# Holding back the splits of the last expert's weights in layer 1 of a two-layer trunk

## The chip, the cores and the metric

The kernel runs on one core of a Trainium2 chip. A core has a matrix engine (TensorE, PE in the profile, with its weight loads listed as PEld), a vector engine (VectorE, DVE), a scalar engine (ScalarE, ACT), a general engine (GpSimd, POOL) and SyncE (SP), which here does nothing but issue transfers. Each works through its own list of instructions in the order of the program. They meet at semaphores, and 16 DMA engines move data between the large memory and the on-chip memory. The metric is the device time of one execution in microseconds (us), as a median of several runs.

## The reference, cut to what matters

Two layers, each a token mixer (attention and gating branches) followed by a mixture of 16 experts. The experts part, for 512 latent and 256 context tokens:

```python
def ec_moe(h, w_r, w1, w3, w2):
    aff = jax.nn.softmax((h @ w_r).astype(jnp.float32), axis=-1)
    gate, idx = lax.top_k(jnp.swapaxes(aff, 1, 2), cap)      # each expert picks its tokens
    xin = jax.vmap(lambda hb, ib: hb[ib])(h, idx)
    hid = jax.nn.silu(jnp.einsum('becd,edf->becf', xin, w1)) * jnp.einsum('becd,edf->becf', xin, w3)
    ye = jnp.einsum('becf,efd->becd', hid, w2) * gate[..., None].astype(h.dtype)
    return jax.vmap(lambda yb, ib: jnp.zeros((n, D), h.dtype).at[ib.reshape(-1)].add(yb.reshape(-1, D)))(ye, idx)
```

The three matrices of an expert are 1024 x 1024 in float32. An expert takes 64 latent and 32 context tokens, 96 rows in all.

## The kernel before, in words

The change lies in `experts_quad`, the experts of the first layer. Each expert's matrices come in as 24 tiles of 128 x 1024 floats (512 KB), eight for each of w_e1, w_e3 and w_e2. The tiles are fetched in one fixed sequence: w_e1 of expert e+1, then w_e2 of expert e, then w_e3 of expert e+1, and so on. So the sequence ends with eight tiles of w_e2 of expert 14, eight of w_e3 of expert 15 and eight of w_e2 of expert 15. `moe_load` issues them from SP as buffers come free. A transfer on SP also waits until the transfer eight places ahead of it has landed, since eight semaphores take turns.

For experts 0 to 14 the loop runs `stage_1(e+1)` (the product with w_e1, 96 matmuls recorded as 192, then a Silu on ACT, line 1329), `stage_h(e)` (the hidden activations of expert e are transposed on PE, line 1316, and copied from PSUM by two ACT copies, line 1323), `stage_2(e)` (the product with w_e2 on PE, line 1267; three gate multiplications on DVE, line 1342, each followed by a scatter that adds its quarter rows to the token table `x1a` from POOL, line 1344), and `stage_3(e+1)` (the product with w_e3, then a multiplication on DVE, line 1335). The three scatters of an expert go one after the other, since all of them add into `x1a`.

The last expert, number 15, is treated apart, because its result is taken straight into the next layer. Its hidden activations are kept as a pair of reduced-precision parts (`fp32r`, high and low): ACT copies the high part from PSUM (line 1320), and DVE subtracts to get the low part (line 1321). Its eight w_e2 tiles are split the same way by `split_w`: a CAST on ACT (line 153) makes the high part and a subtraction on DVE (line 155) the low part, so one tile costs one instruction on each. `mm_rows` (line 1276) then runs six matmuls for a tile: high by high twice, high by low twice, low by high twice. The splits use the tag `w` with six buffers, so three tiles can be split ahead of their matmuls. Around this `stage_x` loads a row of numbers (`k<-in_iota`, line 1364), compares it on DVE (line 1368, called hot below) and reloads `x1a` in six pieces (line 1372). `settle` (line 1381) then adds the last expert by a matmul with that comparison. The next layer begins there, with four early loads of its `w_in` tiles into buffers `y`, `y`, `m`, `m`.

The order on each engine is made by a scheduler that runs ahead of time: an instruction that has what it needs early in its estimate is put early, though written later in the code. `tc.issue_after(ins)` makes the instructions of a block stand behind `ins` on the engine of `ins`; other engines and the waits on data are left alone.

Of the kernel before, what the change touches and what calls it, by code (L numbers as in the profile page):

```python
# [38 lines left out]
def fr(ap):  # L39
    return ap.bitcast(F32)  # L40
# [68 lines left out]
class Trunk:  # L109
# [1145 lines left out]
    def experts_quad(self, l):  # L1255
        nc = self.nc
# [3 lines left out]
        state, got = {}, {}  # L1260
# [9 lines left out]

        def mm_rows(ps, hT, name, e):
            for k in range(KD):
                w = self.moe_w((name, l, e, k))
                for i, (a, b) in enumerate(self.PAIRS):
                    for hf in range(2):
                        nc.tensor.matmul(ps[:, hf * 512:(hf + 1) * 512], lhsT=hT[a][:, k, :],
                                         rhs=w[b][:, hf * 512:(hf + 1) * 512],
                                         start=(k == 0 and i == 0), stop=(k == KD - 1 and i == 2))
# [25 lines left out]
        def stage_h(e, final):  # L1304
            x = state.pop(("s", e))
            if final:
                pair = [self.tl([P, 4, 2, M], F32R, "k3") for _ in range(2)]
                state["h", e] = [v.rearrange("p q f m -> p (q f) m") for v in pair]
            else:
                hT = self.tl([P, 4, 2, M], F32, "k3")  # L1310
                state["h", e] = hT.rearrange("p q f m -> p (q f) m")
            for f in range(2):
                tp = self.p1([P, 3, P])
                for r in range(3):
                    c0 = r * QW + f * P
                    nc.tensor.transpose(tp[:, r, :], x[:, c0:c0 + P], self.ident)
                v = tp.rearrange("p r (q m) -> p q r m", q=4)
                o = lambda t: t[:, :, f, :].rearrange("p q (r m) -> p q r m", r=3)
                if final:
                    nc.scalar.copy(o(pair[0]), v)  # L1320
                    nc.vector.tensor_tensor(out=o(pair[1]), in0=v, in1=fr(o(pair[0])), op=ALU.subtract)
                else:
                    nc.scalar.copy(o(hT), v)  # L1323
# [23 lines left out]
        def stage_2_rows(e):  # L1347
            ps = self.p2([M, D])
            mm_rows(ps, state.pop(("h", e)), "w_e2", e)
            y = self.tl([M, D], F32, "tg")  # L1350
            for hs in (slice(0, BW), slice(BW, D)):
                nc.vector.scalar_tensor_tensor(out=y[:, hs], in0=ps[:, hs], scalar=self.gate[:M, e:e + 1], in1=self.gtr[:M, hs],
                                               op0=ALU.mult, op1=ALU.mult)
            ys = state["y"] = [self.tl([P, D], F32R, "w") for _ in range(2)]
            for hs in (slice(0, BW), slice(BW, D)):
                nc.scalar.copy(ys[0][:M, hs], y[:, hs])
                nc.vector.tensor_sub(ys[1][:M, hs], y[:, hs], fr(ys[0][:M, hs]))
            nc.gpsimd.indirect_dma_start(out=dst[:, :], out_offset=bass.IndirectOffsetOnAxis(ap=self.idx[:M, e:e + 1], axis=0),
                                         in_=y, in_offset=None, compute_op=ALU.add)
# [34 lines left out]
        for e in range(NEXP):  # L1394
            final = e == NEXP - 1
            if not final:
                stage_1(e + 1)
            stage_h(e, final)
            if final:
                stage_x()  # L1400
                stage_2_rows(e)
            else:
                stage_t(e + 2)
                gather(e + 3)
                stage_2(e)
                stage_3(e + 1)
# [314 lines left out]
```

## Time and profile before

| | us |
|---|---|
| median of 3 runs | 2679.74 |
| lowest, highest of them | 2674.07, 2679.84 |
| the profiled execution | 2676.03 |
| span of its instructions | 2674.3 |
| mean granted clock of TensorE, share of full | 0.967 |

The page says for each engine how long it was busy and how often. It then cuts the span into 40 slices of 66.9 us and gives each engine's busy share in tenths. The later views list, for a window, who waited for whom, or the instructions in order of time; an idle time in square brackets names what ended it. Times count from the first instruction of the span.

### The profile page before, as it was taken

The page shows a single profiled execution, that of the slowest core. Times are in us where ns is not written, and L with a number is a line of the kernel's source. Part 1 is how long each engine was busy: PE and PEld are TensorE (multiplying, and loading weights), DVE is VectorE, ACT ScalarE, POOL GpSimd, SP SyncE. Part 2 cuts the span into 40 slices and gives each one's busy share as a digit, 9 for nine tenths or more (in the row PEclk, how much of TensorE's full clock was granted, in tenths as well). Part 3 has the DMA queues.
Part 4 walks back from the last instruction along what each step waited for, and adds up shares of the span by engine and source line. Part 5 has one row for each costly group of instructions (what it writes and reads, how often), then busy time and mean ns, then how long its engine had stood idle before and what let it go on. Part 6 is the DMA issues. An engine that isn't in the chain of part 4 may idle for free.

```text
span 2674.3 us, 47343 instructions
## 1 busy us (share of the span) xinstructions
PE 2448.9 (92%) x19598; PEld 1681.8 (63%) x19598; DVE 1224.4 (46%) x2457; ACT 804.0 (30%) x1729; POOL 190.5 (7%) x188
## 2 busy tenths in 40 slices
PE   7989999999999879999996899999999969988886
PEld 5888877777778746666664587888788843211111
DVE  7767776878696431111111455657765341100002
ACT  4556455444623300000000355534453220000000
POOL 0000000001000011111111100000000011000100
PEclk9999999999999989999998899999999979999999
DMA  7674664342246779999999353252223689999998
GB/s 281 197 231 150 209 208 135 121 146 94 78 146 236 267 284 383 390 386 382 382 385 391 113 173 119 76 166 71 80 78 121 209 336 401 407 408 407 407 406 333
DMA packets 194264, 654.59 MB, mean 245 GB/s; under 512 B 22720, under 2 KB 32960, under 8 KB 194048
## 3 DMA queue, kind: packets, MB, share of 16 engines
q1 hardware_dynamic: 174928, 610.32, 62.3%
q0 software_dynamic: 13696, 27.53, 4.2%
q10 hardware_dynamic: 5424, 13.70, 1.8%
q8 instruction: 154, 2.52, 0.4%
q14 instruction: 62, 0.51, 0.1%
HBM read 615.03 MB, written 25.95 MB: 240 GB/s over the span
## 4 chain that ended last, share of the span: by engine, by line
PE 62%; DMA 20%; DVE 10%; ACT 4%; issue 2%; POOL 1%; SPq 0%; ACTq 0%; POOLq 0%; DVEq 0%
PE p L327 22%; PE p L1267 18%; PE p L467 5%; DMA h<-in_w_e 4%; PE p L1429 4%; PE p L1094 3%; DMA w<-in_w_e 2%; PE p L492 2%; DMA raw<-in_w_in 2%; DVE w L155 2%; DMA q<-q 2%; DMA e<-in_w_e 2%; DMA raw<-in_w_e 2%; DMA m<-in_w_e 2%; PE p L609 1%
## 5 line engine op out<-in xcount | busy, mean ns | idle before, releaser
L327 PE MATMUL p<-h,w 128*128 128x512 f32 (+1 forms) x4416 | 916.4, 358 | 12.3 <-DVE w L155 5.6
L327 PEld LDWEIGHTS p<-h,w 128*128 128x128 f32 x4416 | 709.1, 191 | 131.4 <-issue 7.5
L155 DVE TENSOR_TENSOR w<-raw,w 128x1024 fp32r<-128x1024 f32 x224 | 273.4, 1222 | 227.4 <-ACT w L153 218.3
L153 ACT CAST w<-raw 128x1024 fp32r<-128x1024 f32 x224 | 235.0, 1050 | 374.0 <-PE p L327 140.1
L1267 PE MATMUL p<-h,k 128*32 128x256 f32 x3744 | 205.7, 379 | 0.0
L467 PE MATMUL p<-y,w 128*128 128x512 f32 (+1 forms) x864 | 177.3, 362 | 1.1 <-DVE w L155 1.1
L1267 PEld LDWEIGHTS p<-h,k 128*32 128x32 f32 x3744 | 120.4, 110 | 81.4 <-issue 1.5
L264 DVE SCALAR_TENSOR_TENSOR w<-raw,raw 128x1024 bf16<-128x1024 f32 x128 | 155.7, 1220 | 22.9 <-DMA raw<-in_w_adaT 16.1
L167 POOL TENSOR_TENSOR st<-st,mhalf 128x1 f32<-128x1 f32 x76 | 55.5, 730 | 1544.2 <-DVE st L165 1264.0
L467 PEld LDWEIGHTS p<-y,w 128*128 128x128 f32 x864 | 144.6, 191 | 28.2 <-DVE w L155 1.5
L1329 ACT ACTIVATE v<-p 128x768 f32<-128x768 f32 x16 | 13.0, 812 | 427.0 <-PE p L1267 427.0
L492 PE MATMUL p<-k,q 128*128 128x256 f32 (+1 forms) x576 | 109.5, 320 | 25.7 <-DMA q<-q 15.6
L1429 PE MATMUL p<-h,k 128*64 128x512 f32 x444 | 113.2, 622 | 16.8 <-DMA h<-in_w_e 15.7
L492 PEld LDWEIGHTS p<-k,q 128*128 128x128 f32 x576 | 85.4, 195 | 41.3 <-issue 10.7
L1267 PE MATMUL p<-raw,k 128*32 128x256 f32 x1560 | 88.5, 383 | 21.0 <-ACT k L1323 21.0
L1344 POOL DMA_INDIRECT x1a<-tg,idx x45 | 69.8, 1550 | 440.8 <-DVE tg L1342 238.5
L1462 ACT COPY k<-p 128x256 f32<-128x256 f32 x32 | 10.4, 375 | 297.6 <-PE p L1442 297.6
L1094 PE MATMUL p<-w,h 128*128 128x512 f32 x384 | 91.3, 395 | 1.6 <-DVE w L155 1.1
L1474 DVE TENSOR_TENSOR w<-w,p 128x512 f32<-128x512 f32 x16 | 11.0, 687 | 163.5 <-PE p L1429 152.3
L1429 PEld LDWEIGHTS p<-h,k 128*64 128x64 f32 x444 | 26.2, 137 | 94.6 <-DMA h<-in_w_e 57.4
L1267 PEld LDWEIGHTS p<-raw,k 128*32 128x32 f32 x1560 | 50.5, 111 | 55.2 <-ACT k L1323 21.2
L1335 DVE TENSOR_TENSOR v<-v,p 128x768 f32<-128x768 f32 x16 | 15.3, 954 | 149.4 <-PE p L1267 140.3
(340 smaller groups left out, 3038.0 us busy)
## 6 DMA issues: line engine op xcount, KB each, us to landing
h<-in_w_e SPq DMA_DIRECT2D x267, 512.0 KB
raw<-in_w_in SPq DMA_DIRECT2D x164, 512.0 KB
raw<-in_w_e SPq DMA_DIRECT2D x115, 512.0 KB
e<-in_w_e SPq DMA_DIRECT2D x93, 512.0 KB
y<-in_w_e SPq DMA_DIRECT2D x88, 512.0 KB
m<-in_w_e SPq DMA_DIRECT2D x84, 512.0 KB
raw<-in_w_adaT SPq DMA_DIRECT2D x80, 512.0 KB
w<-in_w_e SPq DMA_DIRECT2D x54, 512.0 KB
```

Source lines behind the costliest of these rows:

```text
L153: nc.scalar.copy(hi, fr(raw))
L155: nc.vector.tensor_sub(lo, fr(raw), fr(hi))
L167: nc.gpsimd.tensor_tensor(out=r, in0=v, in1=self.mhalf, op=ALU.pow)
L264: nc.vector.scalar_tensor_tensor(out=dump, in0=fr(raw), scalar=1.0, in1=self.cb[v], op0=ALU.mult, op1=ALU.mult, accum_out=self.mod[s, l][: ...
L327: nc.tensor.matmul(ps, lhsT=w[a][:, k * P:(k + 1) * P], rhs=h[k][:, b, :], start=(k == 0 and i == 0), stop=(k == KD - 1 and i == 2))
L467: nc.tensor.matmul(bps, lhsT=wb[a][:, (jj * 4 + k) * P:(jj * 4 + k + 1) * P], rhs=y[k][:, b, :], start=(k == 0 and i == 0), stop=(k == 3 a ...
L492: nc.tensor.matmul(ps, lhsT=Q[:, h, i, qs], rhs=k, start=(i == 0), stop=(i == 1))
L609: nc.tensor.matmul(ypsd[pr][64 * hh:64 * hh + 64, b * P:(b + 1) * P], lhsT=V[vi][:, head * 64:(head + 1) * 64], rhs=pT[hh][:, j * P:(j + 1 ...
L1094: nc.tensor.matmul(banks[i][hf], lhsT=c.mh[k][:, a, i * P:(i + 1) * P], rhs=w[b][:, hf * BW:(hf + 1) * BW], start=(k == 0 and p == 0), sto ...
L1267: nc.tensor.matmul(ps[32 * q:32 * q + 32, r * QW:(r + 1) * QW], lhsT=xT[:, k, 32 * r:32 * r + 32], rhs=w[:, q * QW:(q + 1) * QW], start=(k ...
L1344: nc.gpsimd.indirect_dma_start(out=dst4, out_offset=bass.IndirectOffsetOnAxis(ap=self.idx4[:, r, e:e + 1], axis=0), in_=y[:, r, :], in_off ...
L1429: nc.tensor.matmul(ps[half(h), :], lhsT=xT[:, k, :], rhs=w[:, h * BW:(h + 1) * BW], start=(k == 0), stop=(k == KD - 1))
```

## The change

The split of the last expert's w_e2 tiles is traced inside `issue_after` with the last of the two ACT copies of that expert's high part:

```diff
         def mm_rows(ps, hT, name, e):
             for k in range(KD):
-                w = self.moe_w((name, l, e, k))
+                with self.tc.issue_after(state["after"]):
+                    w = self.moe_w((name, l, e, k))
...
                 if final:
-                    nc.scalar.copy(o(pair[0]), v)
+                    state["after"] = nc.scalar.copy(o(pair[0]), v).ins
                     nc.vector.tensor_tensor(out=o(pair[1]), in0=v, in1=fr(o(pair[0])), op=ALU.subtract)
```

The line numbers after the first hunk are one higher in the changed kernel. On ACT, in the kernel before, from the copies of expert 13's hidden activations (`k_2472`) to the fourth split; `v_14916` is the Silu of expert 15, `k_2503` the copies of expert 14, `k_2509` those of expert 15, and `w_15164`, `w_15174`, `w_15184` the high parts of the last expert's first three tiles:

```order
L1323 COPY k_2472_14547<-p_2474_14553 128x4x96
L153 CAST w_15164<-m_14754 128x1024
L153 CAST w_15174<-y_14768 128x1024
L153 CAST w_15184<-y_14782 128x1024
L1329 ACTIVATE v_14916<-p_2497_14811 128x768
L1323 COPY k_2503_14918<-p_2504_14919 128x4x96
L1323 COPY k_2503_14918<-p_2505_14924 128x4x96
L1320 CAST k_2509_15131<-p_2511_15133 128x4x96
L1320 CAST k_2509_15131<-p_2512_15139 128x4x96
L153 CAST w_15194<-y_14796 128x1024
```

And the same stretch of ACT in the changed kernel:

```order
L1324 COPY k_2472_14547<-p_2474_14553 128x4x96
L1330 ACTIVATE v_14916<-p_2497_14811 128x768
L1324 COPY k_2503_14918<-p_2504_14919 128x4x96
L1324 COPY k_2503_14918<-p_2505_14924 128x4x96
L1321 CAST k_2509_15131<-p_2511_15133 128x4x96
L1321 CAST k_2509_15131<-p_2512_15139 128x4x96
L153 CAST w_15164<-m_14754 128x1024
L153 CAST w_15174<-y_14768 128x1024
L153 CAST w_15184<-y_14782 128x1024
L153 CAST w_15194<-y_14796 128x1024
```

Three CASTs moved from ahead of expert 15's Silu to behind the last expert's copies. On DVE, in the kernel before, from expert 14's `stage_3` multiplication (`v_14545`) on; `tg_15026` are the gate multiplications that feed the scatters of expert 14, `k_2514` is hot:

```order
L1335 TENSOR_TENSOR v_14545<-v_14545,p_2488_14697 128x768
L155 TENSOR_TENSOR w_15166<-m_14754,w_15164 128x1024
L155 TENSOR_TENSOR w_15176<-y_14768,w_15174 128x1024
L155 TENSOR_TENSOR w_15186<-y_14782,w_15184 128x1024
L1342 SCALAR_TENSOR_TENSOR tg_15026<-p_2506_14929,gate_114,q_8562 128x256 x3
L1335 TENSOR_TENSOR v_14916<-v_14916,p_2508_15033 128x768
L1321 TENSOR_TENSOR k_2510_15132<-p_2511_15133,k_2509_15131 128x4x96
L1321 TENSOR_TENSOR k_2510_15132<-p_2512_15139,k_2509_15131 128x4x96
L155 TENSOR_TENSOR w_15196<-y_14796,w_15194 128x1024
L1368 TENSOR_SCALAR k_2514_15147<-k_2513_15145,st_15148 96x768
L155 TENSOR_TENSOR w_15206<-y_14812,w_15204 128x1024
```

And in the changed kernel:

```order
L1336 TENSOR_TENSOR v_14545<-v_14545,p_2488_14697 128x768
L1343 SCALAR_TENSOR_TENSOR tg_15026<-p_2506_14929,gate_114,q_8562 128x256 x3
L1336 TENSOR_TENSOR v_14916<-v_14916,p_2508_15033 128x768
L1322 TENSOR_TENSOR k_2510_15132<-p_2511_15133,k_2509_15131 128x4x96
L1322 TENSOR_TENSOR k_2510_15132<-p_2512_15139,k_2509_15131 128x4x96
L155 TENSOR_TENSOR w_15166<-m_14754,w_15164 128x1024
L155 TENSOR_TENSOR w_15176<-y_14768,w_15174 128x1024
L1369 TENSOR_SCALAR k_2514_15147<-k_2513_15145,st_15148 96x768
L155 TENSOR_TENSOR w_15186<-y_14782,w_15184 128x1024
L155 TENSOR_TENSOR w_15196<-y_14796,w_15194 128x1024
```

Hot stood behind four splits and stands behind two. On SP, in the kernel before, from the last two w_e2 tiles on:

```order
L147 DMA e_14854<-in_w_e 128x1024
L147 DMA y_15254<-in_w_in 128x1024
L147 DMA y_15256<-in_w_in 128x1024
L147 DMA m_15258<-in_w_in 128x1024
L1372 DMA e_15151<-x1a 128x1024
L1372 DMA raw_15153<-x1a 128x1024
L1372 DMA raw_15155<-x1a 128x1024
L1372 DMA raw_15157<-x1a 128x1024
L1364 DMA k_2513_15145<-in_iota 96x768
L1372 DMA raw_15159<-x1a 128x1024
L1372 DMA raw_15161<-x1a 128x1024
L147 DMA m_15260<-in_w_in 128x1024
```

And in the changed kernel:

```order
L147 DMA e_14854<-in_w_e 128x1024
L1373 DMA e_15151<-x1a 128x1024
L1373 DMA raw_15153<-x1a 128x1024
L1373 DMA raw_15155<-x1a 128x1024
L1373 DMA raw_15157<-x1a 128x1024
L1365 DMA k_2513_15145<-in_iota 96x768
L1373 DMA raw_15159<-x1a 128x1024
L1373 DMA raw_15161<-x1a 128x1024
L147 DMA y_15254<-in_w_in 128x1024
L147 DMA y_15256<-in_w_in 128x1024
L147 DMA m_15258<-in_w_in 128x1024
L147 DMA m_15260<-in_w_in 128x1024
```

Three loads of the next layer's `w_in`, which reuse buffers of the tiles being split, moved from ahead of the `x1a` loads to behind them. On PE eight small transposes of the next layer (line 174) stand between the matmuls of `mm_rows` and no longer behind them; on POOL nothing moved.

## Rows read from the trace of the kernel before

**Rows 1.** The head of the page and the busy shares of PE in 40 slices.

```profile
span 2674.3 us, 47343 instructions
...
PE   7989999999999879999996899999999969988886
```

**Rows 2.** Who waited for whom from 1445 to 1520 us: in total us, how often, the longest.

```profile
ACT w L153 <- DMA m<-in_w_e: 48.4, 1, 48.4
...
PE p L1267 <- ACT k L1323: 21.0, 1, 21.0
...
DVE k L1368 <- DMA k<-in_iota: 6.8, 1, 6.8
...
PE p L1276 <- DVE w L155: 5.9, 1, 5.9
```

**Rows 3.** ACT in order of time, around experts 13 and 14: start us, duration us, line, operation, names, and in brackets the idle time ahead and what ended it.

```profile
1415.44 0.81 ACT L1329 ACTIVATE v<-p 128x768 f32<-128x768 f32 x1 [31.02 <-PE p L1267]
...
1465.42 1.04 ACT L153 CAST w<-m 128x1024 fp32r<-128x1024 f32 x1 [48.42 <-DMA m<-in_w_e]
...
1467.87 1.04 ACT L153 CAST w<-y 128x1024 fp32r<-128x1024 f32 x1 [0.17 <-DMA y<-in_w_e]
1468.82 0.81 ACT L1329 ACTIVATE v<-p 128x768 f32<-128x768 f32 x1
1469.52 0.85 ACT L1323 COPY k<-p 128x384 f32<-128x384 f32 x2
1494.07 0.86 ACT L1320 CAST k<-p 128x384 fp32r<-128x384 f32 x2 [23.70 <-PE p L1316]
...
1515.07 1.04 ACT L153 CAST w<-y 128x1024 fp32r<-128x1024 f32 x1
```

**Rows 4.** PE in order of time, in the same columns, from expert 13's transposes to the end of the last expert's product.

```profile
1415.30 0.87 PE L1316 MATMUL p<-ident,v 128*128 128x128 f32 x6
...
1416.98 3.23 PE L1267 MATMUL p<-h,k 128*32 128x256 f32 x56
...
1448.19 0.87 PE L1316 MATMUL p<-ident,v 128*128 128x128 f32 x6
1470.05 2.79 PE L1267 MATMUL p<-raw,k 128*32 128x256 f32 x24 [20.98 <-ACT k L1323]
...
1494.60 6.25 PE L1276 MATMUL p<-w,k 128*96 128x512 f32 x26 [0.29 <-ACT k L1320]
1506.70 6.96 PE L1276 MATMUL p<-w,k 128*96 128x512 f32 x22 [5.86 <-DVE w L155]
```

**Rows 5.** The chain of work that ended last, from 1440 to 1510 us: start us, us, what.

```profile
1447.20 10.74 DMA h<-in_w_e
...
1458.01 9.84 DMA y<-in_w_e
...
1498.05 6.83 DMA k<-in_iota
```

**Rows 6.** The transfers of line 147 issued from SP between 1440 and 1480 us: duration of the issue (ns, least, median, most), and the starts of the first and the last.

```profile
L147 SPq DMA_DIRECT2D m<-in_w_e x4: 327/328/328, 1451.0 to 1455.5; - x4
L147 SPq DMA_DIRECT2D y<-in_w_e x4: 327/328/328, 1456.7 to 1460.5; - x4
L147 SPq DMA_DIRECT2D e<-in_w_e x3: 327/327/328, 1461.8 to 1464.2; - x3
```

**Rows 7.** DVE in order of time, in the columns of rows 3.

```profile
1427.61 1.27 DVE L1342 SCALAR_TENSOR_TENSOR tg<-p,gate,q 128x256 f32<-128x256 f32 x3 [8.67 <-PE p L1267]
1438.04 0.95 DVE L1335 TENSOR_TENSOR v<-v,p 128x768 f32<-128x768 f32 x1 [9.16 <-PE p L1267]
...
1482.01 1.27 DVE L1342 SCALAR_TENSOR_TENSOR tg<-p,gate,q 128x256 f32<-128x256 f32 x3 [11.84 <-PE p L1267]
1492.42 0.95 DVE L1335 TENSOR_TENSOR v<-v,p 128x768 f32<-128x768 f32 x1 [9.15 <-issue]
```

**Rows 8.** The scatters of line 1344 on POOL in order of time, in the columns of rows 3, and last the time of all 45 from issue to landing (us, least, median, most).

```profile
1428.50 1.54 POOL L1344 DMA_INDIRECT x1a<-tg,idx  x1 [14.51 <-DVE tg L1342]
1437.38 1.54 POOL L1344 DMA_INDIRECT x1a<-tg,idx  x1 [7.34 <-DMA x1a<-tg,idx]
1446.02 1.54 POOL L1344 DMA_INDIRECT x1a<-tg,idx  x1 [7.09 <-DMA x1a<-tg,idx]
1482.77 1.54 POOL L1344 DMA_INDIRECT x1a<-tg,idx  x1 [35.21 <-DVE tg L1342]
1487.33 1.54 POOL L1344 DMA_INDIRECT x1a<-tg,idx  x1 [3.02 <-DMA x1a<-tg,idx]
1492.31 1.54 POOL L1344 DMA_INDIRECT x1a<-tg,idx  x1 [3.44 <-issue]
...
DMA to landing us min/median/max: 3.8/7.9/8.7
```

**Rows 9.** The first transfer that SP issued after 1495 us.

```profile
1496.19 0.33 SPq L1372 DMA_DIRECT2D e<-x1a  x1
```

**Rows 10.** Stretches of the program: their length, busy us of PE, PEld, DVE, ACT and POOL with counts, the granted clock of TensorE (1.00 is full), the share of the DMA engines, and GB/s.

```profile
1505.00:1510.00 5.00, 3.30 (x8) 2.26 (x9) 4.93 (x5) 1.04 (x1) 0.00 (x0) 0.50 0.63 257
...
1565.00:2000.00 435.00, 424.26 (x2479) 353.31 (x2479) 272.19 (x545) 210.43 (x506) 12.89 (x20) 1.00 0.34 106
```

## The prediction, made before the result was known

> **What bounds the kernel now.** I read the head of the page first. PE is busy in nearly every slice, so time is won only where PE itself stands still. The slice from 1404 to 1471 us shows a 6 between nines [rows 1]. I then asked who waited for whom around it: PE waited 21.0 us for an ACT copy, and ACT had waited 48.4 us for a weight tile, a wait far longer than any of the others; later PE waited 5.9 us for a split on DVE, and DVE 6.8 us for `k<-in_iota` [rows 2].
>
> ACT in order of time tells the rest. Expert 14's Silu started 0.14 us after expert 13's transposes on PE had begun (1415.30 to 1415.44) [rows 3, 4]. Expert 14's transposes began at 1448.19, but expert 15's Silu started at 1468.82. Ahead of it stood three CASTs whose tiles came in at 1465.4 to 1467.9 [rows 3, 4]. The Silu needed none of them. The tiles are the first three of the last expert's w_e2, which PE wants only at 1494.60. So the wait is a queue on ACT and not the weights of the product that PE was to do next.
>
> Are those weights there? A transfer issued at 1447.20 let the one at 1458.01 go, eight places on, and that one landed at 1467.85; so eight tiles take 9.84 to 10.74 us, about 1.29 us a tile [rows 5]. The first split tile is the last of four `m` loads [rows 6] and was there at 1465.42 [rows 3]. Counted back by 1.29, the eighth tile of w_e3 of expert 15 is there at 1464.1 and its first at 1455.1, and w_e2 of expert 14 from 1444.8 to 1453.8. All of these were issued while PE stood, so PE's progress does not set them.
>
> **The change part by part.** *The Silu goes ahead.* It can start at 1448.19 + 0.14 = 1448.33. From Silu to the first matmul takes 1470.05 - 1468.82 = 1.23 us [rows 3, 4], so PE begins expert 14's w_e2 product at 1449.56, 20.49 us earlier. It uses a tile every 1.3 us, the eighth at about 1458.7 and the eighth of w_e3 at about 1469: both at least 4.9 us after they land. From start to gate multiplication took 10.63 us for expert 13 (1416.98 to 1427.61) and 11.96 us for expert 14 (1470.05 to 1482.01) [rows 4, 7]; PE ran slower for the first microseconds after its long idle. Without the idle I take 10.63: 1460.19. In the same way the w_e3 product's multiplication, 21.06 us after the start (1416.98 to 1438.04), comes at 1470.62 where it came at 1492.42 [rows 4, 7]. That step alone gains 21.8 us.
>
> *The splits lose their head start.* Three CASTs of 1.04 us now follow the copies. The copies start 1494.07 - 1492.42 = 1.65 us after the multiplication [rows 3, 7], at 1472.27, and last 0.86 us; the first matmul then waits for a CAST, until 1474.2 instead of 1472.8. That is 1.4 us, and the first low part needs some 1.2 us more on DVE. The eight small transposes now fill part of it; where they stood they lay under DVE's gate multiplication and cost nothing. All this is hidden by the next wait; without that cover it would cost 2.6 us.
>
> *The row of numbers becomes the bound.* Hot on DVE stands behind two splits now. Everything from the third low part on waits for `k<-in_iota`. That load is behind the `x1a` loads on SP, and the first of those waits for the third scatter of expert 14. The chain goes: gate multiplication 1460.19; first scatter 0.89 us later (1427.61 to 1428.50 [rows 7, 8]), 1461.08; second scatter when the first has landed. Beside weight traffic these steps took 8.88 and 8.64 us, without it 4.56 and 4.98 [rows 8]. The last weight tile is issued at 1464.2 [rows 6] and lands about 9.84 later, 1474.0. So the first step is a loaded one, 8.64: 1469.7. The second runs half beside traffic that is ending, and I take 6.0, between 4.98 and 8.64 and nearer the free one: 1475.7. The third lands free, 1496.19 - 1492.31 = 3.88 us [rows 8, 9]: 1479.6. The load is issued 1498.05 - 1496.19 = 1.86 us later and lands after 6.83 us [rows 5, 9], at 1488.3, where it landed at 1504.88.
>
> *The end of the product.* Before, matmuls resumed 1506.70 - 1504.88 = 1.82 us after the landing [rows 4, 5], with hot and one subtraction between, as they will now: 1490.1. Then 22 of 48 were left; now, with two tiles done and two high-by-high matmuls of the third, 34 are left. The 22 took 6.96 us, part of it at the lower clock after the wait: the five microseconds from 1505 show a granted clock of 0.50, which is the 1.2 GHz level [rows 4, 10]. The 12 more at 6.25 / 26 = 0.24 us add 2.9 us [rows 4]. The product ends at 1490.1 + 9.86 = 1500.0, where it ended at 1513.66. The gain is 13.7 us.
>
> *The moved loads* (`y`, `y`, `m`) are issued behind six `x1a` loads and the row. Before, this group kept the DMA engines busy until some 1508 (0.63 of the five microseconds from 1505 [rows 10]), 12 us after its first issue. With three tiles more at 1.29 us it takes 16 us from 1479.6: 1495.5. The first split of such a tile was at 1515.07, 1.4 us after the product [rows 3], so now at 1501.4. It is covered by 5.9 us; without cover the excess would be paid in full.
>
> Nothing else moves on any engine, and from 1565 to 2000 us PE is busy 424 of 435 us with the DMA engines at 0.34 [rows 10], so a start that is earlier by 13.7 us stays earlier to the end. Against its own time of 2676.03 the sum is 2662.3. The median shown is 3.7 us higher, and I put the forecast a little above the sum: 2663.5.
>
> **Bounds.** What the trace does not show is the scatter chain when traffic ends in the middle of it. With the two steps free, 4.56 and 4.98, it ends 5.1 us earlier and the gain is 18.8 us. With two loaded steps of 8.88 and the slowest landing, 8.7 [rows 8], it ends at 1461.08 + 17.76 + 8.7 = 1487.5, 7.9 us later, and the gain is 5.8 us.
>
> **A rule of the skill on the row's load.** The row took 6.83 us, with four 512 KB loads of `x1a` ahead of it and three transfers behind; now six stand behind [rows 5, 9]. The Trainium skill (DMA: Bandwidth & Descriptors, "Queues, rings and completion order") says that each DMA engine takes the descriptors of a ring in order. By that the transfers behind cost it nothing, as in my sum. If they shared the engines evenly with it, three more of 1.29 us would make it 3.9 us later, and the gain 9.8 us.
>
> **Rivals.** (a) The chain is the free one: gain near 18.8, 2657. For it speaks that the weights end at 1474 at the latest; against it that the first scatter falls wholly beside them.
> (b) The chain stays loaded to its end, or the load shares: gain 5.8 to 10, about 2668. The median of 45 scatters, 7.9 us, speaks for it [rows 8]; against it that the last three, without weights, took half. The Trainium skill (the same page and section) says that an engine goes in turns between queues that have work, which would slow the scatters exactly as long as weights are left. By that too the third one is free.
> (c) The wait for the row takes the place of the wait removed: the landing does not follow PE's earlier start and stays at 1504.88. Then the product has 12 more matmuls behind it and the kernel is slower by 2.9 us: 2678.9 by the profiled time. The point from which it decides is a landing later than 1502.0; each microsecond past that costs one. Against it: even the fully loaded chain lands the row at 1487.5 + 1.86 + 6.83 = 1496.2.
> (d) The edit does not do what it says, PE waiting for weights at 1449 in any case: no gain, 2677. Against it are the landings of 1444.8 to 1453.8 counted above.
>
> **How the numbers follow.** Forecast 0.68 (gain 10 to 17 us), (a) 0.10, (b) 0.14, (c) 0.04, (d) 0.04. A measurement of this kernel tells about 0.3% from no change, 8.0 us. The forecast, (a) and about two thirds of (b) are faster by more: 0.87. The rest of (b), (d) and most of (c) lie within it: 0.11. Slower by more needs (c) with a landing some 5 us later than before: 0.02. The range runs from (a)'s end, 2655.5, to 2671, a gain of 8.7 by the median shown, and leaves out the rest of (b), (c) and (d).
>
> **What would show it.** In the changed profile the 21 us of PE idle near 1449 is gone and ACT's Silu follows the transposes by about 0.14 us. The idle inside the last expert's product (5.86 before) grows to some 11 us and ends with DVE's third split behind hot. Three scatters lie 8 to 9, 5 to 7 and 4 us apart up to the first `x1a` load, and the split of the first `w_in` tile is not waiting for a transfer. I am wrong if PE still stands after 1449, if the first `w_in` split waits, or if the row lands after 1493.

## The result, and the profile after

The changed kernel takes 2663.74 us (median of 4 runs, 2660.60 to 2667.70), the kernel before, measured beside it, 2679.36 us (4 runs, 2674.07 to 2679.84). The ratio is 0.9947, with a 95% interval of 0.9933 to 0.9962: faster by half a per cent. The profiled execution after took 2664.36 us, 11.67 less than that of before. Line numbers behind the edit are one higher than before.

The head of the page, with PE in 40 slices. The 6 between nines of [rows 1] stands one slice further on now, from 1464 to 1531 us:

```profile
span 2662.6 us, 47346 instructions
...
PE   7998999999999979999999699999999969888886
```

Who waited for whom, from 1430 to 1515 us:

```profile
DVE k L1369 <- DMA k<-in_iota: 13.7, 1, 13.7
...
PE p L1277 <- DVE w L155: 13.5, 1, 13.5
...
PE p L1267 <- ACT k L1324: 0.5, 1, 0.5
```

Of [rows 2], ACT's wait of 48.4 us for a weight tile is gone, and PE's 21.0 us behind it is 0.5. The two that had been small have more than doubled: DVE waits 13.7 us for the row of numbers (6.8 before) and PE 13.5 us for the third split (5.9). So 20.5 us were won and 7.6 us given back inside the next product, and PE has 1.5 us more to wait for the first split: 11.4 us in all.

ACT in order of time, the counterpart of [rows 3]:

```profile
1447.84 0.81 ACT L1330 ACTIVATE v<-p 128x768 f32<-128x768 f32 x1 [31.33 <-PE p L1267]
...
1471.77 0.86 ACT L1321 CAST k<-p 128x384 fp32r<-128x384 f32 x2 [22.37 <-PE p L1317]
1472.65 1.04 ACT L153 CAST w<-m 128x1024 fp32r<-128x1024 f32 x1
...
1502.99 1.04 ACT L153 CAST w<-y 128x1024 fp32r<-128x1024 f32 x1
```

PE, the counterpart of [rows 4]:

```profile
1447.70 0.87 PE L1317 MATMUL p<-ident,v 128*128 128x128 f32 x6
1449.07 1.50 PE L1267 MATMUL p<-raw,k 128*32 128x256 f32 x24 [0.50 <-ACT k L1324]
...
1473.75 0.69 PE L1277 MATMUL p<-w,k 128*96 128x512 f32 x2 [1.75 <-ACT w L153]
...
1491.63 9.96 PE L1277 MATMUL p<-w,k 128*96 128x512 f32 x34 [13.49 <-DVE w L155]
```

The Silu follows the transposes by 0.14 us and PE goes on 1.37 us after they began. The first split stands behind the copies. After two tiles and the first two matmuls of the third the product stops until 1491.63, and ends at 1491.63 + 9.96 = 1501.59, 53.9 us after the transposes, where it was 1513.66 - 1448.19 = 65.5 us.

POOL's scatters of expert 14, the counterpart of [rows 8]:

```profile
1460.47 1.54 POOL L1345 DMA_INDIRECT x1a<-tg,idx  x1 [13.24 <-DVE tg L1343]
1468.88 1.54 POOL L1345 DMA_INDIRECT x1a<-tg,idx  x1 [6.87 <-DMA x1a<-tg,idx]
1476.97 1.54 POOL L1345 DMA_INDIRECT x1a<-tg,idx  x1 [6.55 <-DVE w L155]
```

SP's issues behind them, the counterpart of [rows 9]:

```profile
1480.73 0.33 SPq L1373 DMA_DIRECT2D e<-x1a  x1
...
1482.64 0.35 SPq L1365 DMA_DIRECT2D k<-in_iota  x1
...
1484.06 7.88 SPq L147 DMA_DIRECT2D y<-in_w_in  x2
```

DVE, from expert 14's gate multiplication to the third split, the counterpart of [rows 7]:

```profile
1459.71 1.27 DVE L1343 SCALAR_TENSOR_TENSOR tg<-p,gate,q 128x256 f32<-128x256 f32 x3 [21.21 <-PE p L1267]
...
1489.83 0.62 DVE L1369 TENSOR_SCALAR k<-k,st 96x768 fp32r<-96x768 f32 x1 [13.74 <-DMA k<-in_iota]
1490.36 3.48 DVE L155 TENSOR_TENSOR w<-y,w 128x1024 fp32r<-128x1024 f32 x3
```

The steps of the chain are 8.41 us, 8.09 us, then 3.76 us to the first `x1a` load, 1.91 us to the row's issue and 7.19 us until hot starts. The third scatter is listed as released by DVE, but what it must wait for in the program is the second scatter's landing; a releaser is inferred. The last weight tile was the load issued from SP at 1464.1; the transfers issued from 1463.9 to 1465 us, with the time to landing last:

```profile
e<-in_w_e SPq DMA_DIRECT2D x1, 512.0 KB, 12.2
```

It landed near 1476.3.

The stretches in which the chain runs, in the columns of [rows 10] (the last two numbers are the DMA share and GB/s, the one ahead of them the granted clock):

```profile
1468.00:1470.00 2.00, 2.00 (x40) 0.91 (x29) 0.00 (x0) 0.00 (x0) 1.12 (x1) 1.00 0.67 266
1470.00:1472.00 2.00, 0.87 (x6) 0.64 (x6) 0.95 (x1) 0.23 (x1) 0.42 (x1) 1.00 0.78 236
1472.00:1474.00 2.00, 0.25 (x2) 0.24 (x2) 1.29 (x3) 1.98 (x4) 0.00 (x0) 1.00 0.47 155
1474.00:1476.00 2.00, 2.00 (x13) 1.54 (x12) 2.00 (x2) 1.84 (x3) 0.00 (x0) 1.00 0.16 41
1476.00:1478.00 2.00, 2.00 (x10) 1.26 (x8) 0.09 (x1) 1.66 (x2) 1.03 (x1) 1.00 0.00 0
...
1490.00:1495.00 5.00, 3.37 (x8) 2.32 (x9) 4.93 (x5) 1.04 (x1) 0.00 (x0) 0.50 0.97 342
```

The weight traffic thins out from 1468 and is all but gone by 1476. The last line shows PE restarting at the 1.2 GHz level after its 13.5 us of idle; it fits that these 34 matmuls took 9.96 us, where the same 34 took 8.10 us behind a stop of only 0.37 us in row_first_again below, at a granted clock of 1.00.

### The profile page after: what moved, and what is told of

Its sections match the earlier page's. It is cut to its first block, busy times and chain, and to the rows that moved or that the text cites. A ratio compares the mean times of both kernels' runs of the same rounds, so it can differ in the third digit from the quotient of the medians.

```text
span 2662.6 us, 47346 instructions
## 1 busy us (share of the span) xinstructions
PE 2447.3 (92%) x19598; PEld 1681.8 (63%) x19598; DVE 1223.9 (46%) x2457; ACT 804.1 (30%) x1729; POOL 190.3 (7%) x188
## 5 line engine op out<-in xcount | busy, mean ns | idle before, releaser
L1343 DVE SCALAR_TENSOR_TENSOR tg<-p,gate,q 128x256 f32<-128x256 f32 x45 | 19.0, 478 | 142.7 <-PE p L1267 142.7
## 6 DMA issues: line engine op xcount, KB each, us to landing
h<-in_w_e SPq DMA_DIRECT2D x267, 512.0 KB, 10.9
raw<-in_w_e SPq DMA_DIRECT2D x115, 512.0 KB, 10.5
y<-in_w_e SPq DMA_DIRECT2D x88, 512.0 KB, 10.5
```

## The experiments

To set profiles beside each other in spite of a start that differs by some microseconds from one execution to the next, I use the stage's length: from expert 14's transposes to the next layer's first matmul of line 327 (331 in one kernel), both read from PE in order of time. Each ratio is to the kernel before, measured beside it.

| kernel | what differs | stage, us | median, us (before) | ratio, 95% |
|---|---|---|---|---|
| before | | 88.7 | | |
| after | splits held | 77.2 | 2663.74 (2679.36) | 0.9947, 0.9933 to 0.9962 |
| row_first | after, row ahead of `x1a` | 67.9 | 2650.84 (2678.88) | 0.9897, 0.9881 to 0.9912 |
| hold14 | held until expert 14's copy | 80.4 | 2669.56 (2678.88) | 0.9962, 0.9949 to 0.9976 |
| before_row_first | before, row ahead of `x1a` | 80.5 | 2671.21 (2678.88) | 0.9971, 0.9959 to 0.9983 |
| one_free | after, one split not held | 92.0 | 2677.58 (2678.88) | 0.9996, 0.9987 to 1.0005 |
| row_early | after, row from ACT's queue | 70.9 | 2657.84 (2678.39) | 0.9919, 0.9906 to 0.9933 |
| lo_late | after, splits behind hot | 83.2 | 2670.08 (2678.39) | 0.9966, 0.9953 to 0.9979 |
| after_again | after, unchanged | 78.2 | 2667.51 (2678.39) | 0.9960, 0.9947 to 0.9974 |
| row_early_held | row_early, next splits held | 62.2 | 2648.06 (2674.95) | 0.9903, 0.9886 to 0.9920 |
| row_first_again | row_first, unchanged | 68.8 | 2654.64 (2674.95) | 0.9922, 0.9906 to 0.9939 |

**Is the wait for the row what bounds the stage now?** In row_first the row is loaded ahead of the `x1a` pieces, so that it no longer waits for the scatters.

```diff
-            nc.sync.dma_start(row, self.t["iota"][:n].partition_broadcast(M))
+            first = nc.sync.dma_start(row, self.t["iota"][:n].partition_broadcast(M)).ins
...
-                nc.sync.dma_start(x, dst[i * P:(i + 1) * P, :])
+                with self.tc.issue_after(first):
+                    nc.sync.dma_start(x, dst[i * P:(i + 1) * P, :])
```

> The changed kernel, with the load of the row of numbers issued on SP ahead of the x1a loads and no longer behind four of them. Theory (after the change the last expert's product is bound by that row, which waits for the third scatter): the idle of 13.5 us inside the product goes, the product runs at the pace of PE and ends about 12 us after its first matmul, near 1486.5 instead of 1501.6; the kernel takes about 2649.5 us, 1.1% less than before the change. Rival (the splits, made on ACT and DVE only after the copies, are what paces the product): PE still waits for each split, the product ends after 1493, and the kernel takes 2655 us or more.

It took 2650.84 us. SP in order of time:

```profile
1463.30 0.97 SPq L1365 DMA_DIRECT2D k<-in_iota  x1
1475.52 0.34 SPq L1374 DMA_DIRECT2D e<-x1a  x1
```

PE behind its stop in the product:

```profile
1476.82 9.38 PE L1277 MATMUL p<-w,k 128*96 128x512 f32 x34 [4.57 <-DVE w L155]
```

The scatters are as slow as they were (8.69 and 8.46 us), and the stop in the product is 4.6 us instead of 13.5. So the stop is the row's, and the chain of scatters mattered only because the row stood behind it. The theory had it gone altogether, but the row took 11.7 us until hot here, and the product 18.3 us from its first matmul and not 12. The rival, that the pace of the splits is what holds the product, falls: nothing was done to them here, and behind that one stop PE ran all 34 matmuls without another. One side effect of the edit: two `m` loads of `w_in` went out ahead of the row (from 1461.58 us), where in the changed kernel they come last.

> row_first once more, beside row_early_held on the same chip, since its first profile started expert 14 some 6 us earlier than the other kernels did. Theory (the stage alone gains 21.1 us against the kernel before, the rest was luck of the runs): ratio 0.991 to 0.993. Rival (the earlier start belongs to the kernel): 0.990 or less, as measured first.

PE in row_first_again:

```profile
1479.10 8.10 PE L1277 MATMUL p<-w,k 128*96 128x512 f32 x34 [0.37 <-DVE w L155]
...
1494.30 8.16 PE L1383 MATMUL p<-w,k 96*128 96x512 f32 x22 [4.34 <-ACT w L1357]
```

The repeat gave a ratio of 0.9922, as its theory said, and a stop of 0.37 us; PE lost 4.3 us later on, in `settle`, behind a split of the next layer's `w_in` tile that had not landed. Its median lay 20.3 us below before, and its stage was 19.9 us shorter. The first median lay 28.0 us below before with a stage only 20.9 us shorter; the difference was not found again.

**Are the two waits apart?** before_row_first makes the same edit in the kernel before.

> The kernel before the change, with the row's load alone moved ahead of the x1a loads. Theory: PE's idle of 21 us before expert 14's product stays as it was, the idle of 5.9 us inside the last product goes with the clock that it cost, the product ends near 1506.3 instead of 1513.7: 2668.5 to 2671 us. Rival (the two edits remove one and the same wait): as the first run, below 2655 us, or no gain at all.

PE in order of time:

```profile
1467.08 2.79 PE L1267 MATMUL p<-raw,k 128*32 128x256 f32 x24 [20.23 <-ACT k L1323]
...
1491.82 11.33 PE L1276 MATMUL p<-w,k 128*96 128x512 f32 x48 [0.30 <-ACT k L1320]
```

The early idle of 20.2 us stays and the product runs through. The stage is 8.2 us shorter than before; the change alone makes it 11.5 shorter, and the two together 20.9 and 19.9, about their sum of 19.7. The time, 2671.21 us, is just past the end of the range that the theory gave (2671). Two waits, one behind the other, each with its own price.

**Does one held-up instruction do it?** In one_free only the first of the eight tiles is split without being held.

```diff
-                with self.tc.issue_after(state["after"]):
+                if k == 0:
                     w = self.moe_w((name, l, e, k))
+                else:
+                    with self.tc.issue_after(state["after"]):
+                        w = self.moe_w((name, l, e, k))
```

> The changed kernel, with the first of the eight splits let go as before and seven held. Theory (the Silu stands in a queue behind a CAST that waits for its tile, so one CAST is nearly as bad as three): the Silu starts about 1 us after the first tile's landing, near 1466, PE stands idle for some 18 us before expert 14's product, and the kernel takes about 2674.5 us, 2 us less than before. Rival (each of the three CASTs costs a share of its own): two thirds of the gain are kept, about 2668 us.

ACT in order of time:

```profile
1463.02 1.04 ACT L153 CAST w<-m 128x1024 fp32r<-128x1024 f32 x1 [48.38 <-DMA m<-in_w_e]
1463.97 0.80 ACT L1333 ACTIVATE v<-p 128x768 f32<-128x768 f32 x1
```

PE behind it:

```profile
1465.20 2.79 PE L1267 MATMUL p<-raw,k 128*32 128x256 f32 x24 [18.49 <-ACT k L1327]
```

A single CAST ahead of the Silu brings back 18.5 of the 21 us, and the whole gain is lost (2677.58 us, not to be told from before, and 3 us above what was expected). The two other tiles came in 1.2 us apart [rows 3] and cost only the rest, while without their head start the later stop grew to 8.8 us.

**Could the splits have kept a head start?** hold14 holds them only until expert 14's own activations are copied, one stage earlier.

```diff
                 if final:
-                    state["after"] = nc.scalar.copy(o(pair[0]), v).ins
+                    nc.scalar.copy(o(pair[0]), v)
...
                 else:
-                    nc.scalar.copy(o(hT), v)
+                    state["after"] = nc.scalar.copy(o(hT), v).ins
```

> The changed kernel, with the splits held back only behind the copies of expert 14's activations, so that the Silu and the copies go first and three tiles are split during the products of experts 14 and 15. Theory (what counts is the scatter chain that ends in the row's landing): the three subtractions now stand on DVE ahead of the gate multiplication of expert 14 and wait for their tiles until about 1467.5, so the multiplication moves from 1459.7 to about 1470, the first scatter with it, the row lands near 1493 and the product ends near 1502 although it has 12 matmuls fewer to do by then: about 2664.5 us, as the changed kernel. Rival (a head start of the splits is a gain once ACT is free): the product ends 2.9 us earlier than in the changed kernel, 2661 us.

DVE in order of time:

```profile
1465.44 1.23 DVE L155 TENSOR_TENSOR w<-m,w 128x1024 fp32r<-128x1024 f32 x1 [26.10 <-ACT w L153]
1466.69 2.44 DVE L155 TENSOR_TENSOR w<-y,w 128x1024 fp32r<-128x1024 f32 x2
1469.05 1.26 DVE L1343 SCALAR_TENSOR_TENSOR tg<-p,gate,q 128x256 f32<-128x256 f32 x3
```

POOL's scatters:

```profile
1469.80 1.54 POOL L1345 DMA_INDIRECT x1a<-tg,idx  x1 [21.66 <-DVE tg L1343]
1477.74 1.54 POOL L1345 DMA_INDIRECT x1a<-tg,idx  x1 [6.40 <-DMA x1a<-tg,idx]
1482.70 1.54 POOL L1345 DMA_INDIRECT x1a<-tg,idx  x1 [3.42 <-issue]
```

The same fault, one engine further: the three subtractions stand on DVE ahead of expert 14's gate multiplication and wait for the same tiles. That multiplication comes 20.50 us after the transposes instead of 12.01, and everything behind it with it. PE's stop in the product:

```profile
1497.63 7.98 PE L1277 MATMUL p<-w,k 128*96 128x512 f32 x22 [18.29 <-DVE w L155]
```

So the head start gains nothing, as the theory said. The time, 2669.56 us, is 5 us above the 2664.5 that it gave, but the ratio, 0.9962, is not to be told from the changed kernel's 0.9947 and 0.9960. By the stage hold14 is 2.2 to 3.2 us longer than the changed kernel; this fits the first scatter, which still fell beside traffic and took 7.94 us, 3.4 more than the 4.56 of a free one [rows 8].

**Why was the second scatter slow?** The trace of after names a split as what released the third scatter. In lo_late all splits stand behind hot, so DVE is free while the scatters run.

```diff
-                with self.tc.issue_after(state["after"]):
+                with self.tc.issue_after(state["after"]), self.tc.issue_after(state["hot_at"]):
                     w = self.moe_w((name, l, e, k))
...
-            nc.vector.tensor_scalar(hot, row, col[:M, :], None, op0=ALU.is_equal)
+            state["hot_at"] = nc.vector.tensor_scalar(hot, row, col[:M, :], None, op0=ALU.is_equal).ins
```

> The changed kernel, with the low parts on DVE held behind hot as well, so that DVE does nothing while the second and third scatters of expert 14 are on their way. Theory (the second scatter took 8.1 us and not 6.0 because the DMA engines still had weight tiles to move): the step from the second to the third scatter stays at 8 us, the row lands as in the changed kernel, and with 46 of 48 matmuls left behind it in place of 34 the product ends about 2.9 us later: 2666.5 us. Rival (DVE's subtractions hold up the scatter, since the profile names DVE as the one that released it): the step falls to 5 to 6 us, the row lands 2 to 3 us earlier, and the time is that of the changed kernel.

> The changed kernel once more, to size the gain beside runs of the kernel before on the same chip. The two profiled executions differ by 11.7 us, the medians by 15.6 us. Theory (the gain is what the chain of this stage gives, 11.6 us from the transposes to the end of the product): ratio 0.9950 to 0.9960. Rival (something outside the stage gains too, 13.7 us or more): ratio 0.9949 or less.

POOL's scatters in lo_late:

```profile
1459.90 1.54 POOL L1345 DMA_INDIRECT x1a<-tg,idx  x1 [13.34 <-DVE tg L1343]
1468.37 1.54 POOL L1345 DMA_INDIRECT x1a<-tg,idx  x1 [6.92 <-DMA x1a<-tg,idx]
1476.70 1.54 POOL L1345 DMA_INDIRECT x1a<-tg,idx  x1 [6.79 <-issue]
```

The same in after_again:

```profile
1461.08 1.54 POOL L1345 DMA_INDIRECT x1a<-tg,idx  x1 [13.33 <-DVE tg L1343]
1469.61 1.54 POOL L1345 DMA_INDIRECT x1a<-tg,idx  x1 [6.99 <-DMA x1a<-tg,idx]
1476.77 1.64 POOL L1345 DMA_INDIRECT x1a<-tg,idx  x1 [5.61 <-DVE w L155]
```

With DVE idle from 1472.96 to 1491.11 the second step is 8.33 us, so DVE has nothing to do with it. In the changed kernel's second profile it is 7.16 us. The head start of two splits is worth most of what lo_late loses: its 46 matmuls behind the row take 13.57 us where the 34 of after took 9.96. Its stage is 5.0 to 6.0 us longer than the changed kernel's, of which up to 1.5 us are the row's own slower transfer; its median lies 2.6 us above that of after_again beside it, where 2.9 were expected. The ratio of after_again, 0.9960, is at the edge of its theory's range, and its interval reaches into the rival's: whether something outside the stage gains too is not settled.

**Can the row leave SP's order altogether?** row_early issues the row from ACT's queue, behind expert 14's copies, so that SP's order no longer touches it.

```diff
+        def stage_row():
+            row = state["row"] = self.tl([M, 8 * M], F32, "k3")
+            nc.scalar.dma_start(row, self.t["iota"][:8 * M].partition_broadcast(M))
+
         def stage_x():
             n = 8 * M
-            row = self.tl([M, n], F32, "k3")
-            nc.sync.dma_start(row, self.t["iota"][:n].partition_broadcast(M))
+            row = state["row"]
...
             stage_h(e, final)
+            if e == NEXP - 2:
+                stage_row()
```

> The changed kernel, with the row of numbers loaded from ACT's queue behind the copies of expert 14, so that neither the scatters nor the next layer's tiles stand ahead of it (in row_first it landed 9.8 us after the gate's copies and PE still stood idle for 4.6 us). Theory: the row is there before hot is due, PE runs the last product without a stop of more than 1 to 2 us, about 12.5 us from its first matmul to its end where the changed kernel took 27.9 and row_first 18.3: some 2645 us, 1.25% less than before the change. Rival (without the row's wait the six x1a loads behind the third scatter become the bound): the product ends early but settle waits for its x1a tiles, and the time is that of row_first, 2650 us.

PE in order of time:

```profile
1473.96 10.87 PE L1277 MATMUL p<-w,k 128*96 128x512 f32 x46
...
1496.49 7.60 PE L1385 MATMUL p<-w,k 96*128 96x512 f32 x22 [8.86 <-ACT w L1357]
```

ACT in the same stretch:

```profile
1485.70 0.62 ACT L1357 CAST w<-tg 96x512 fp32r<-96x512 f32 x1 [4.41 <-DVE tg L1353]
1494.87 1.04 ACT L153 CAST w<-y 128x1024 fp32r<-128x1024 f32 x1 [8.55 <-DMA y<-in_w_in]
1495.82 0.61 ACT L1357 CAST w<-tg 96x512 fp32r<-96x512 f32 x1
```

The product has no stop at all, but most of what it won is lost in `settle`, and the time (2657.84) is 13 us above what was expected. The rival named the place, `settle`, but not the cause. It is the change's own subject again: the CAST of a `w_in` tile that has not landed stands on ACT ahead of the second CAST of line 1357. So row_early_held holds those splits until the normalization's square of the last of the first four token tiles, which comes later on ACT.

```diff
-        return self.split_w(self.load_w(key) if raw is None else raw)
+        if raw is None:
+            return self.split_w(self.load_w(key))
+        with self.tc.issue_after(self.squared):
+            return self.split_w(raw)
...
         for x in xs:
-            self.norm_tile(x)
+            self.squared = self.norm_tile(x)
...
```

> row_early, with the splits of the next layer's early w_in tiles held on ACT behind the squares of the first four token tiles. In row_early the last product ended 38.6 us after expert 14's transposes began (53.9 in the changed kernel), but then PE stood idle for 8.9 us, because a CAST that waited for a w_in tile stood on ACT ahead of the high part that settle needs. Theory (it is the same queue on ACT as in the kernel before): that idle goes, and the kernel takes 8 to 9 us less than row_early, 2647 to 2650 us. Rival (the x1a and w_in tiles themselves come too late, so that the wait only moves behind the squares): no more than 3 us less than row_early, 2655 us.

PE in order of time:

```profile
1472.06 10.85 PE L1281 MATMUL p<-w,k 128*96 128x512 f32 x46
...
1485.18 8.73 PE L1389 MATMUL p<-w,k 96*128 96x512 f32 x23 [0.22 <-DVE w L1362]
```

The 8.9 us are gone, the stage takes 62.2 us where row_early's took 70.9, and 2648.06 us is the lowest median here. Beside row_first_again, measured with it, its six runs (2646.23 to 2651.98) lie below that kernel's six (2651.87 to 2658.75) but for 0.11 us. Against the kernels measured at other times the ratios tell less: 0.9903 is not told from the first 0.9897 of row_first, and its interval overlaps that of row_early (0.9919).

## Why the prediction was right, and where it was off

**The Silu goes ahead: right.** The Silu came 0.14 us after the transposes (0.14 forecast), PE went on after 1.37 (1.37), the gate multiplication came after 12.01 us (12.00). That the weights were there, counted back tile by tile, holds: PE had no stop in that product. The reason given, that all of them were issued while PE stood, was misread: PE ran until 1449.06 and only four of the 16 loads were issued later, but the two kernels do the same up to there. So rival (d) is out; one_free shows the cause directly.

**The splits lose their head start: right.** The first matmul of the product came 2.62 us after the transposes of line 1317 (1473.75 - 1471.13), and the wait for the row hid it.

**The row of numbers becomes the bound: right in kind, one term too small.** Against the sum: gate to first scatter 0.76 (0.89), first step 8.41 (8.64), second step 8.09 (6.0), to the `x1a` load 3.76 (3.88), to the row's issue 1.91 (1.86), the row's transfer 7.19 (6.83). Together +2.0 us, and the second step alone is +2.1. The step that failed is therefore "the second runs half beside traffic that is ending, and I take 6.0": it was priced by how much traffic was left on average, and it paid as a loaded one. In the three profiles with this timing it was 8.09, 7.16 and 8.33, never near the free 4.98. A second figure in that step was off as well: the last weight tile, put at 1464.2 + 9.84 = 1474.0, landed 12.2 us after its issue, near 1476.3. With it 2.3 us later, the second scatter had less free time than the sum gave it.

**The end of the product: right.** Matmuls resumed 1.80 us behind hot's start (1.82), and the 34 took 9.96 us (9.86). The stop was 13.5 us (some 11), longer by the scatter's step and an earlier first matmul. The product ended 53.9 us after the transposes instead of the forecast 1500.0 - 1448.19 = 51.8: a gain of 11.6 us by the stage where 13.7 was forecast.

**The moved loads: covered, by another path.** The first split was not waiting for a transfer (1502.99). But the second `y` load was issued only when the third split's subtraction ended: 1484.06 + 7.88 - 0.33 = 1491.61, against 1490.36 + 1.22 = 1491.58 on DVE (in after_again 1492.83 against 1492.81). The `m` loads behind it, issued at 1492.03 and after, took 5.4 us at the median and so landed near 1498, later than the 1495.5 us of the sum and still ahead of the split. Row_early shows what that cover hid: 8.9 us once the product no longer stops, 4.3 us in row_first_again. "Without cover the excess would be paid in full" is shown there.

**The rivals.** (a), a free chain, and (c), a landing that does not follow, are refuted by the same rows; what spoke for (a), weights that end at 1474 at the latest, did not hold. (b), the loaded chain, is nearer than I gave it: its second step was loaded, its third landing free. Of the Trainium skill's rule in "Queues, rings and completion order" (DMA: Bandwidth & Descriptors) this case decides nothing: only three transfers, not six, had been issued behind the row when it landed, as many as before, and its transfer to hot's start took 7.19, 8.45 and 8.71 us in after, after_again and lo_late with the same four ahead.

**The time.** 2663.74 against 2663.5 is closer than the reasoning was. The profiled executions differ by 11.7 us, where the sum had 13.7; the medians by 15.6, and in the repeat by 10.9 (2678.39 - 2667.51). The agreement of the median within 0.3 us is chance.

## What to carry to other kernels

An engine that works in order stops at an instruction whose operand has not landed, however many ready ones stand behind it: look at a long wait for a transfer, and ask what the next instruction on that engine would have needed. The same fault was met three times here, on ACT before the change, on DVE in hold14 and on ACT again in row_early, each time by splitting weights early. When such a wait goes, price what is queued ahead of the next one (here a 288 KB row behind loads that waited for scatters): moving that single load made the stage 8.2 to 9.4 us shorter, the change itself 10.5 to 11.5.

## What the runs showed that was not expected

The second scatter of expert 14 was issued while weight traffic was thinning out, and paid nearly the full loaded price (7.16 to 8.33 us in the changed kernel and lo_late). The next scatter came at 1476.97, 1476.77 and 1476.70 us in after, after_again and lo_late, and at 1477.74 behind hold14's first, in each within some 2 us of the fall of the DMA share to 0.1 to 0.3, whether the scatter ahead had been issued 7.2 or 8.3 us earlier. It looks as if it lands with the last of the traffic, not after a share of it. But the share holds the scatter's own packets too; from 1474 to 1476 us in after they were (queue, packets, MB, share of 16 engines):

```profile
q0 software_dynamic: 28, 0.02, 7.9%
```

The loads moved 17 packets in these two microseconds. Of the second scatter's 144 packets 65 moved from 1470 to 1472, 51 from 1472 to 1474 and these 28 after that; the third, without loads beside it, moved all 144 between 1478 and 1481. So the time was lost while the packets moved. In after_again, with the shortest step, no packet of the loads moved after 1475 us, while in after and lo_late some still did; but what spread the scatter's packets out is not shown, for no run moved the end of the traffic by itself.

The row issued early, beside weight traffic, took 11.7 us until hot's start in row_first and 9.5 in row_first_again, longer than the 7.2 to 8.7 it took behind four `x1a` loads. It was still the better place: hot started 33.2 and 31.0 us after expert 14's transposes, in the changed kernel 42.1 and 42.8.
